# Second MLP matmul of a two-layer encoder: weight sums by accumulating DMA, and seven products for its last piece too

## The chip, the cores and the metric

One core of a Trainium2 chip. The time is that of one execution on the device, in microseconds (us): the median of three executions, and beside it one execution that the hardware profiler recorded.

## The reference

Two encoder layers on 512 tokens of 1024 features in fp32. Each layer is a token mixer (dilated window attention in layer 0, latent attention in layer 1) and a dense MLP with 4096 hidden units. The change touches the MLP alone, above all its second product:

```
def sq_relu_mlp(h, w1, w2):
    a = jax.nn.relu(h @ w1)
    return (a * a) @ w2

x = x + y                      # y: the mixer's output
h = rms_norm(x, norm_ffn[i])
x = x + sq_relu_mlp(h, ffn_w1[i], ffn_w2[i])
```

After layer 0 the next mixer begins with a norm over the 1024 features of each token, so it needs whole rows of `x`.

## The kernel before

Every matmul of two fp32 matrices is made from three matmuls in a shorter format (fp32r): each operand is split into a rounded part (`hi`, a copy on ScalarE) and a remainder (`lo`, a subtraction on VectorE), and hi x hi, hi x lo and lo x hi are added up in PSUM. So each piece of 128 x 1024 weights or activations costs one ScalarE copy and one VectorE subtraction before TensorE can use it. For the weights these are L157 and L158 (`load_unit`) or L523 and L524 (`split_w`, in `wino`); for the activations of the second MLP matmul L485 and L486 (`split_a`). Tiles named `whi`, `wlo` and `asp` hold the results. `whi` and `wlo` have four buffers each, `asp` four, raw weights three.

The MLP runs in four chunks of 1024 hidden units. `up(ch, grp)` makes one half chunk of hidden units from the normed input (matmuls L184, 192 of 128 x 512 for a half chunk); at its end four groups of 128 hidden units leave PSUM one after the other, each by a relu (L604) and a square (L605) on ScalarE, into the tile `a2`. `down(ch)` multiplies a chunk's `a2` by its 1024 x 1024 piece of the second weight matrix and adds the result to the residual `resid`. The order of the pieces is written out in `mlp`: two halves of `up(0)`, then for chunks 0 to 2 the first half of the next `up`, `down` of this chunk, the second half of the next `up`; at the end `down_last(3)`.

`down` is `wino` (L489): a 2 x 2 block scheme with seven products of half size (256 tokens x 512 hidden x 512 columns) in place of eight. Each product is 24 matmuls of 128 x 512, made in PSUM banks `sc` (chain a) or `tp` (chains b and d). `Aq(i, j)` is the block of token half i and hidden half j. The table `ORDER` lists the products, whether they open a bank or go on in it, and which block of `resid` gets the bank added afterwards (L553). The left sides of products 5, 6, 3 and 7 are sums or differences of blocks (L518, tile `S`); the weight sides of products 5, 6, 7 and 4 are differences of weight blocks, made by VectorE in place (L513, eight operations of 128 x 1024 for each `wino`). The weights come by eight DMAs of 512 KB from SyncE's queue into the four slots of `wqs`.

`down_last(3)` multiplies the last chunk directly: 192 matmuls (L184), in two column halves. All four left sides are split blocks of `a2`, hidden half 0 first. In the second column half the four token tiles end one after the other: L631 adds a tile to `resid` and calls `done(r, c)`. In layer 0 `done` is `done0`, which, for c = 1, norms the tile for the next mixer (`norm_tile`: mean square on ScalarE L136, a small add on VectorE L128, a power on GpSimd L131, the product L212 on VectorE, eight transposes on TensorE L123 into two `tp` banks, and each bank read by a ScalarE copy L220 and a VectorE subtraction L221). In layer 1 `done` sends the block to the output.

Behind layer 0's MLP the next mixer begins: its first weights (`w_in`, 896 elements in a row of a unit), and small tables `cgB` and `sgB` made by GpSimd (L699 to L701) from a gain `gr` that is loaded once TensorE is done with the last `up`.

A scheduler places the instructions of each engine in an order of its own, from the program's order and a model of costs; an engine runs its instructions in that order.

Of the kernel before, what the change touches and what calls it, by code (L numbers as in the profile page):

```python
# [13 lines left out]
ALU = mybir.AluOpType  # L14
# [73 lines left out]
def encoder_kernel(ctx: ExitStack, tc: tile.TileContext, x, norm_mix, norm_ffn, a_w_qkv, a_q_gain, a_k_gain,  # L88
# [394 lines left out]
    def split_a(x, pool):  # L483
        t = pool.tile([P, 4, 2, 256], F32R, tag="asp", name=nm("asp"), bufs=4)
        A.activation(t[:, :, 0], x, AF.Copy)  # L485
        V.tensor_tensor(t[:, :, 1], x, t[:, :, 0].bitcast(F32), op=ALU.subtract)  # L486
        return t

    def wino(tag, Aq, w, wqs, pool, resid):  # L489

        v = w.rearrange("(k p) c -> p k c", p=P)
        raw, S = {}, {}

        def load(key, slot):
            ki, ni = key  # L500
            raw[key] = []
            for u in range(2):
                t = wqs[:, 2 * slot + u]
                k0 = 4 * ki + 2 * u
                nc.sync.dma_start(t, v[:, k0:k0 + 2, 512 * ni:512 * ni + 512])
                raw[key].append(t)
        for key, slot in zip(((0, 0), (0, 1), (1, 1), (1, 0)), SLOTS[tag % 2]):
            load(key, slot)
        b11, b12, b22, b21 = raw[0, 0], raw[0, 1], raw[1, 1], raw[1, 0]

        def sub(o, x, y):
            for u in range(2):
                V.tensor_tensor(o[u], x[u], y[u], op=ALU.subtract)  # L513

        def stmp(name, x, y, op):
            if name not in S:
                S[name] = pool.tile([P, 4, 256], F32, tag="S", name=nm("S"), bufs=2)
            V.tensor_tensor(S[name], x, y, op=op)  # L518

        def split_w(x):  # L520
# [3 lines left out]
            V.tensor_tensor(lo, x, hi.bitcast(F32), op=ALU.subtract)  # L524
            return hi, lo

        def operands(p):
            if p == 1:
                return Aq(0, 0), b11
            if p == 5:  # L530
                stmp("c", Aq(1, 0), Aq(1, 1), ALU.add)
                sub(b11, b12, b11)
                return S["c"], b11
            if p == 6:
                stmp("c", S["c"], Aq(0, 0), ALU.subtract)
                sub(b11, b22, b11)
                return S["c"], b11
            if p == 3:
                stmp("c", Aq(0, 1), S["c"], ALU.subtract)
                return S["c"], b22  # L540
            if p == 7:
                stmp("d", Aq(0, 0), Aq(1, 0), ALU.subtract)
                sub(b12, b22, b12)
                return S["d"], b12
            if p == 2:
                return Aq(0, 1), b21
            sub(b11, b21, b11)
            return Aq(1, 1), b11

        def add_to(i, n, banks):  # L550
            for t in range(2):
                sl = resid[:, 2 * i + t, 512 * n:512 * n + 512]
                V.tensor_tensor(sl, sl, banks[t], op=ALU.add)  # L553

        banks = {}
        for p, chain, first, adds in ORDER:
# [6 lines left out]
            for u in range(2):  # L563
                hi, lo = split_w(wq[u])
                for t in range(2):
                    for j in range(2):
                        k = 2 * u + j
                        ah = at[:, k, 0, t * P:(t + 1) * P]
                        al = at[:, k, 1, t * P:(t + 1) * P]
                        for i, (lt, rt) in enumerate(((ah, hi), (ah, lo), (al, hi))):  # L570
                            PE.matmul(bk[t], lhsT=lt, rhs=rt[:, j], start=(first and k == 0 and i == 0),  # L571
                                      stop=(k == 3 and i == 2), skip_group_check=True)
            for i, n in adds:
                add_to(i, n, bk)

    SLOTS = ((0, 1, 2, 3), (2, 1, 3, 0))

    ORDER = [(1, "a", True, [(0, 0)]), (5, "b", True, [(1, 1)]), (6, "a", False, [(0, 1)]),
             (3, "b", False, [(0, 1)]), (7, "a", False, [(1, 1)]), (2, "d", True, [(0, 0)]), (4, "a", False, [(1, 0)])]

    def mlp(layer, w1, w2, hT_m, resid, pool, done):
        a2s = {}
# [26 lines left out]
        def down(ch):  # L609
            a2 = a2s.pop(ch)  # L610
            wino(layer * 4 + ch, lambda i, j: a2[:, 4 * j:4 * j + 4, 256 * i:256 * i + 256],
                 w2[1024 * ch:1024 * ch + 1024, :], wqs, pool, resid)

        def down_last(ch):

            a2 = a2s.pop(ch)
            at = {}
            for j in range(2):
                for i in range(2):
                    at[i, j] = split_a(a2[:, 4 * j:4 * j + 4, 256 * i:256 * i + 256], pool)  # L620

            def mm(r, kt, hi, lo, hv):
                t = at[r // 2, kt // 4][:, kt % 4]
                ah, al = (t[:, c, (r % 2) * P:(r % 2) * P + P] for c in range(2))
                sl = slice(0, 512)
                return [(ah, hi, sl), (ah, lo, sl), (al, hi, sl)]

            for c in range(2):
                def evac(r, acc, c=c):
                    sl = resid[:, r, 512 * c:512 * c + 512]  # L630
                    V.tensor_tensor(sl, sl, acc, op=ALU.add)  # L631
                    done(r, c)
                run_block(w_units(w2[1024 * ch:1024 * ch + 1024, :], 512 * c, 512), [1] * 4 if c == 0 else [4], 512,
                          mm, evac)
# [321 lines left out]
```

## Time and profile before

| | us |
|---|---|
| median of three executions | 1455.67 (1455.12 to 1456.37) |
| the profiled execution | 1457.98 |
| its span, first to last instruction | 1456.2 |
| TensorE busy | 1422.8 |
| VectorE busy | 903.5 |
| ScalarE busy | 710.3 |
| GpSimd busy | 117.4 |

The profile names the engines PE (TensorE matmul), PEld (its weight loads), DVE (VectorE), ACT (ScalarE), POOL (GpSimd) and SP (SyncE, which issues the DMAs). A row of the timeline has the start, the length of one or of several instructions that follow each other, engine, line, operation, output and inputs, the count, and in brackets the idle time ahead and what ended it. A row of a group has, behind the bar, its busy time, the mean length of one in ns, and the idle time ahead with its causes. "L184" is line 184 of the kernel.

### The profile page before, as it was taken

The numbers are of one execution on the slowest core, as the hardware profiler recorded it, in microseconds if no ns is written. First come the engines' busy times: TensorE is split into PE (matmuls) and PEld (weight loads), VectorE is DVE, ScalarE is ACT, GpSimd is POOL, SyncE is SP. The second block draws the span as 40 slices with busy tenths as digits, with TensorE's granted clock in tenths as the row PEclk, the third lists the DMA queues.
The fourth block names the chain that finished last, engine by engine and source line by source line (L and its number), as shares of the span: only waits on it lengthen the run. The fifth ranks groups of instructions, "written<-read, shape, count | busy, mean of one in ns | idle before, by whom it ended". The sixth has DMA issues, their size and how long they took to land.

```text
span 1456.2 us, 19181 instructions
## 1 busy us (share of the span) xinstructions
PE 1422.8 (98%) x7164; PEld 1210.6 (83%) x7164; DVE 903.5 (62%) x1431; ACT 710.3 (49%) x1572; POOL 117.4 (8%) x133
## 2 busy tenths in 40 slices
PE   7999999999999999999999999999999999999998
PEld 6889889889988878888888888776778888888887
DVE  6765466556437655285776835688754286675832
ACT  5544455355335533553644543787633453544530
POOL 1120120011011100000000010322100000000000
PEclk9999999999999999999999999999999999999999
DMA  6325114322531334415151032300014305151031
GB/s 227 102 55 167 59 46 131 102 63 58 171 94 58 95 130 157 147 36 171 40 174 58 15 111 68 97 30 30 30 44 162 127 30 173 44 172 61 7 111 72
DMA packets 113053, 135.58 MB, mean 93 GB/s; under 512 B 7488, under 2 KB 72256, under 8 KB 112960
## 3 DMA queue, kind: packets, MB, share of 16 engines
q1 hardware_dynamic: 112960, 134.35, 29.5%
q8 instruction: 57, 0.93, 0.3%
q14 instruction: 36, 0.29, 0.1%
HBM read 130.13 MB, written 4.19 MB: 92 GB/s over the span
## 4 chain that ended last, share of the span: by engine, by line
PE 94%; ACT 3%; DVE 2%; issue 1%; DMA 0%; POOL 0%; SPq 0%; DVEq 0%; ACTq 0%
PE acc L184 64%; PE sc L571 9%; PE tp L571 7%; PE tp L123 4%; PE acc L867 1%; PE sc L761 1%; PE acc L843 1%; PE sco L440 1%; PE sco L444 1%; PE sc L351 1%; PE sc L843 1%; DVE wlo L158 1%; PE sc L344 0%; PE tp L867 0%; PE sc L340 0%
## 5 line engine op out<-in xcount | busy, mean ns | idle before, releaser
L184 PE MATMUL acc<-whi,hT 128*128 128x512 f32 (+2 forms) x1600 | 486.5, 379 | 5.5 <-DVE t L311 2.2
L158 DVE TENSOR_TENSOR wlo<-raw,whi 128x1024 fp32r<-128x1024 f32 (+3 forms) x186 | 215.3, 1162 | 297.5 <-ACT whi L157 296.5
L157 ACT ACTIVATE whi<-raw 128x1024 fp32r<-128x1024 f32 (+3 forms) x186 | 187.2, 1010 | 317.8 <-PE acc L184 256.6
L184 PEld LDWEIGHTS acc<-whi,hT 128*128 128x128 f32 x1600 | 296.3, 189 | 47.1 <-issue 2.9
L184 PE MATMUL acc<-hT_f,whi 128*128 128x512 f32 (+1 forms) x1152 | 322.7, 367 | 1.7 <-DVE resid L650 1.2
L184 PE MATMUL acc<-wlo,hT 128*128 128x512 f32 (+2 forms) x800 | 299.9, 375 | 0.0
L184 PEld LDWEIGHTS acc<-hT_f,whi 128*128 128x128 f32 x1152 | 209.1, 189 | 37.4 <-DVE resid L650 1.6
L184 PE MATMUL acc<-hT_f,wlo 128*128 128x512 f32 (+1 forms) x576 | 208.3, 366 | 0.0
L184 PEld LDWEIGHTS acc<-wlo,hT 128*128 128x128 f32 x800 | 151.3, 189 | 19.9 <-DVE wlo L158 0.5
L523 ACT ACTIVATE whi<-wqs 128x1024 fp32r<-128x1024 f32 x84 | 89.2, 1062 | 110.2 <-PE sc L571 42.6
L184 PEld LDWEIGHTS acc<-hT_f,wlo 128*128 128x128 f32 x576 | 109.0, 189 | 17.5
L571 PE MATMUL sc<-whi,asp 128*128 128x512 f32 x384 | 122.1, 389 | 0.0
L524 DVE TENSOR_TENSOR wlo<-wqs,whi 128x1024 fp32r<-128x1024 f32 x84 | 102.6, 1222 | 25.9 <-ACT whi L523 25.8
L131 POOL TENSOR_TENSOR qrs<-rs_v,nhalf 128x4 f32<-128x4 f32 x48 | 61.5, 1290 | 408.3 <-DVE rs_v L128 393.8
L571 PE MATMUL tp<-whi,asp 128*128 128x512 f32 x288 | 91.6, 389 | 0.0
L571 PEld LDWEIGHTS sc<-whi,asp 128*128 128x128 f32 x384 | 72.1, 188 | 14.9
L184 PE MATMUL acc<-whi,asp 128*128 128x512 f32 x256 | 78.9, 389 | 0.0
L571 PE MATMUL sc<-wlo,asp 128*128 128x512 f32 x192 | 74.7, 389 | 0.0
L571 PEld LDWEIGHTS tp<-whi,asp 128*128 128x128 f32 x288 | 54.0, 188 | 11.2
L136 ACT ACTIVATE junk<-acc 128x128 f32<-128x128 f32 x192 | 53.0, 276 | 18.9 <-PE acc L184 13.9
L513 DVE TENSOR_TENSOR wqs<-wqs 128x1024 f32<-128x1024 f32 x48 | 58.0, 1219 | 0.2
L184 PEld LDWEIGHTS acc<-whi,asp 128*128 128x128 f32 x256 | 48.1, 188 | 10.0
(191 smaller groups left out, 1895.4 us busy)
## 6 DMA issues: line engine op xcount, KB each, us to landing
raw<-in_ffn_w_dram SPq DMA_DIRECT2D x80, 512.0 KB, 3.7
raw<-in_a_w_qkv_dram SPq DMA_DIRECT2D x96, 256.0 KB, 3.4
wqs<-in_ffn_w_dram SPq DMA_DIRECT2D x48, 512.0 KB, 4.4
raw<-in_a_w_qkv_dram SPq DMA_DIRECT2D x64, 192.0 KB, 2.8
raw<-in_a_w_o_dram SPq DMA_DIRECT2D x8, 512.0 KB, 4.1
raw<-in_b_w_o_dram SPq DMA_DIRECT2D x8, 512.0 KB, 3.7
xt<-in_x_dram SPq DMA_DIRECT2D x8, 256.0 KB, 5.6
vd<-vt SPq DMA_DIRECT2D x8, 256.0 KB, 3.5
```

The lines of the kernel that those rows point to most:

```text
L123: PE.transpose(o, i, ident)
L131: G.tensor_tensor(out, v[:, :n], nhalf[:, :n], op=ALU.pow)
L136: A.activation(junk, x, AF.Square, scale=1.0 / math.sqrt(dim), accum_out=out)
L157: A.activation(hi[:, :nk, :n], raw[:, :nk, :n], AF.Copy)
L158: V.tensor_tensor(lo[:, :nk, :n], raw[:, :nk, :n], hi[:, :nk, :n].bitcast(F32), op=ALU.subtract)
L184: PE.matmul(accs[o][:, oc], lhsT=lt, rhs=rt, start=(kt == 0 and p_i == 0 and hv == 0), stop=(kt == total - 1 and p_i == 2), skip_group_che ...
L351: PE.matmul(sc[:, r * P:(r + 1) * P], lhsT=qT[:, r * P:(r + 1) * P], rhs=kT[:, r * P:(r + 1) * P], start=True, stop=True)
L513: V.tensor_tensor(o[u], x[u], y[u], op=ALU.subtract)
L523: A.activation(hi, x, AF.Copy)
L524: V.tensor_tensor(lo, x, hi.bitcast(F32), op=ALU.subtract)
L571: PE.matmul(bk[t], lhsT=lt, rhs=rt[:, j], start=(first and k == 0 and i == 0), stop=(k == 3 and i == 2), skip_group_check=True)
L843: PE.matmul(sc, lhsT=lt, rhs=rt, start=(i == 0), stop=(i == 4))
```

## The change

`wino` gets another set of seven products in another order (5, 1, 3, 6, 7, 2, 4), in which every weight side is a single block or a sum of two blocks with positive signs. The signs move to the left sides (four operations, L517) and to the adds to `resid`, which are now adds or subtractions (`put`, L554). A sum of two weight blocks is no longer made on VectorE: one block is loaded by SyncE's queue as before (L511), and the other is added onto it in SBUF by a DMA that accumulates, issued by GpSimd (`accum_op`, L509). Each `wino` now has ten loads by SyncE and eight accumulating DMAs by GpSimd, each of 512 KB; the eight subtractions of L513 are gone. Slot `sT` of `wqs` is summed onto three times: (0,0)+(0,1) for product 5, then (1,1) for product 6 and (1,0) for product 4, each once the split of the product before is done. The slots change places in a round of four.

`down_last` is removed; the last chunk goes through `wino` too, with `done` passed on. For this call product 4 runs token tile by token tile (`tail`), and `done` is called at each final add (after products 6, 7, 2 and 4); `done0` now norms a tile at its second call.

```diff
-        def operands(p):
-            if p == 1:
-                return Aq(0, 0), b11
-            if p == 5:
-                stmp("c", Aq(1, 0), Aq(1, 1), ALU.add)
-                sub(b11, b12, b11)
-                return S["c"], b11
...
-            sub(b11, b21, b11)
-            return Aq(1, 1), b11
+        def fetch(slot, key, add=False):
...
+                if add:
+                    nc.gpsimd.dma_start(t, src, accum_op=ALU.add)
+                else:
+                    nc.sync.dma_start(t, src)
...
+        sT, s1, s3, s7 = slots
+        fetch(sT, (0, 0))
+        bT = fetch(sT, (0, 1), add=True)
+        b1 = fetch(s1, (0, 0))
+        b3 = fetch(s3, (1, 1))
+        fetch(s7, (0, 1))
+        b7 = fetch(s7, (1, 1), add=True)
+
+        def operands(p):
+            if p == 5:
+                return stmp("c", Aq(1, 0), Aq(1, 1), ALU.subtract), bT
+            if p == 1:
+                return Aq(0, 0), b1
+            if p == 3:
+                stmp("d", S["c"], Aq(0, 0), ALU.subtract)
+                return stmp("c", S["d"], Aq(0, 1), ALU.add), b3
+            if p == 6:
+                return S["d"], fetch(sT, (1, 1), add=True)
+            if p == 7:
+                return stmp("c", Aq(0, 0), Aq(1, 0), ALU.subtract), b7
+            if p == 2:
+                return Aq(0, 1), fetch(s1, (1, 0))
+            return Aq(1, 1), fetch(sT, (1, 0), add=True)
+
+        def put(i, n, op, banks):
             for t in range(2):
                 sl = resid[:, 2 * i + t, 512 * n:512 * n + 512]
-                V.tensor_tensor(sl, sl, banks[t], op=ALU.add)
+                V.tensor_tensor(sl, sl, banks[t], op=op)
+                if done is not None and p in (2, 4, 6, 7):
+                    done(2 * i + t, n)
...
+            tail = done is not None and p == 4
+            parts = {}
+            for u, t in ((0, 0), (1, 0), (0, 1), (1, 1)) if tail else ((0, 0), (0, 1), (1, 0), (1, 1)):
...
-    ORDER = [(1, "a", True, [(0, 0)]), (5, "b", True, [(1, 1)]), (6, "a", False, [(0, 1)]),
-             (3, "b", False, [(0, 1)]), (7, "a", False, [(1, 1)]), (2, "d", True, [(0, 0)]), (4, "a", False, [(1, 0)])]
+    ORDER = [(5, "b", True, (1, 1, ALU.add)), (1, "a", True, (0, 0, ALU.add)), (3, "b", False, (0, 1, ALU.add)),
+             (6, "a", False, (0, 1, ALU.subtract)), (7, "a", False, (1, 1, ALU.subtract)),
+             (2, "d", True, (0, 0, ALU.add)), (4, "a", False, (1, 0, ALU.add))]
...
-        def down_last(ch):
...
-        down_last(3)
+        down(3)
...
         def done0(r, c):
-            if c == 0:
+            state[r] = state.get(r, 0) + 1
+            if state[r] < 2:
                 return
```

Two places show what moves. The first is the end of layer 0's last `up`. TensorE before (`acc_1204` is the last tile of `up`, `asp_1217` a split left side of hidden half 0):

```order
L184 MATMUL acc_1204_7224<-hT_f0_4965,wlo_1216_7318 128x512
L184 MATMUL acc_1204_7224<-hT_f0_4965,whi_1215_7317 128x512 x2
L184 MATMUL acc_1204_7224<-hT_f0_4965,wlo_1216_7318 128x512
L184 MATMUL acc_1221_7365<-whi_1226_7371,asp_1217_7353 128x512
L184 MATMUL acc_1221_7365<-wlo_1227_7372,asp_1217_7353 128x512
```

TensorE now (`asp_1218` is product 5's left side, `asp_1225` product 1's; `tp` and `sc` are the banks of their chains):

```order
L184 MATMUL acc_1204_7230<-hT_f0_4965,whi_1215_7323 128x512 x2
L184 MATMUL acc_1204_7230<-hT_f0_4965,wlo_1216_7324 128x512
L578 MATMUL tp_1219_7376<-whi_1221_7378,asp_1218_7373 128x512
L578 MATMUL tp_1219_7376<-wlo_1222_7379,asp_1218_7373 128x512
L578 MATMUL tp_1220_7377<-whi_1221_7378,asp_1218_7373 128x512
L578 MATMUL tp_1220_7377<-wlo_1222_7379,asp_1218_7373 128x512
L578 MATMUL sc_1226_7415<-whi_1228_7417,asp_1225_7412 128x512
```

ScalarE at the same place, before (`a2_1141` holds the last chunk's activations, L157 copies weights):

```order
L157 ACTIVATE whi_1235_7461<-raw_1234_7459 128x1024
L604 ACTIVATE a2_1141_6801<-acc_1204_7224 128x512
L605 ACTIVATE a2_1141_6801<-a2_1141_6801 128x512
L485 ACTIVATE asp_1219_7359<-a2_1141_6801 128x4x256
L485 ACTIVATE asp_1220_7362<-a2_1141_6801 128x4x256
```

ScalarE now (relu and square are L615 and L616; `S_1217` is product 5's difference):

```order
L523 ACTIVATE whi_1230_7433<-wqs_955_5335 128x1024
L615 ACTIVATE a2_1141_6801<-acc_1204_7230 128x512
L616 ACTIVATE a2_1141_6801<-a2_1141_6801 128x512
L485 ACTIVATE asp_1218_7373<-S_1217_7371 128x4x256
L485 ACTIVATE asp_1225_7412<-a2_1141_6801 128x4x256
```

Before, the first left side behind `up` was split long ago; now it is the one that is made last, behind relu, square and VectorE's difference, and TensorE's four matmuls of product 5 stand ahead of product 1's.

The second place is the end of layer 0's MLP on VectorE, before (L631 adds a finished token tile, L212 is the norm's product, L221 the remainder of a transposed bank):

```order
L631 TENSOR_TENSOR resid_4957<-resid_4957,acc_1237_7493 128x512
L128 TENSOR_SCALAR rs_v_1257_7552<-nss_1255_7549 128x1
L212 SCALAR_TENSOR_TENSOR xn_1256_7550<-resid_4957,nrs_1258_7554,g_mix1_1253_7546 128x1024
L631 TENSOR_TENSOR resid_4957<-resid_4957,acc_1238_7494 128x512
L128 TENSOR_SCALAR rs_v_1263_7599<-nss_1261_7596 128x1
L212 SCALAR_TENSOR_TENSOR xn_1262_7597<-resid_4957,nrs_1264_7601,g_mix1_1253_7546 128x1024
L631 TENSOR_TENSOR resid_4957<-resid_4957,acc_1239_7495 128x512
L221 TENSOR_TENSOR hT_1254_7548<-tp_1259_7557,hT_1254_7548 128x4x128
```

VectorE now (`tp_1249`, `tp_1250` are product 2's banks, `sc_1226`, `sc_1227` product 4's; `wlo_1298`, `wlo_1301` and `w0` are weights of the next mixer):

```order
L554 TENSOR_TENSOR resid_4957<-resid_4957,tp_1250_7574 128x512
L158 TENSOR_TENSOR wlo_1295_7782<-raw_1293_7779,whi_1294_7781 128x2x448
L128 TENSOR_SCALAR rs_v_1259_7614<-nss_1257_7611 128x1
L554 TENSOR_TENSOR resid_4957<-resid_4957,sc_1226_7415 128x512
L128 TENSOR_SCALAR rs_v_1265_7637<-nss_1263_7634 128x1
L212 SCALAR_TENSOR_TENSOR xn_1258_7612<-resid_4957,nrs_1260_7616,g_mix1_1255_7608 128x1024
L212 SCALAR_TENSOR_TENSOR xn_1264_7635<-resid_4957,nrs_1266_7639,g_mix1_1255_7608 128x1024
L158 TENSOR_TENSOR wlo_1298_7788<-raw_1296_7785,whi_1297_7787 128x2x448
L554 TENSOR_TENSOR resid_4957<-resid_4957,sc_1227_7416 128x512
L158 TENSOR_TENSOR w0_7768<-raw_1334_7993,w0_7768 128x512
L158 TENSOR_TENSOR wlo_1301_7794<-raw_1299_7791,whi_1300_7793 128x2x448
L221 TENSOR_TENSOR hT_1256_7610<-tp_1261_7619,hT_1256_7610 128x4x128
```

And TensorE there now (L123 are transposes, the `acc_1286` rows the next mixer's first matmuls):

```order
L578 MATMUL sc_1227_7416<-whi_1272_7671,asp_1269_7658 128x512
L123 MATMUL tp_1261_7619<-ck_89,xn_1258_7612 128x128 x4
L123 MATMUL tp_1262_7626<-ck_89,xn_1258_7612 128x128 x4
L184 MATMUL acc_1286_7769<-whi_1291_7775,hT_1256_7610 128x448
L184 MATMUL acc_1286_7769<-wlo_1292_7776,hT_1256_7610 128x448
L123 MATMUL tp_1267_7642<-ck_89,xn_1264_7635 128x128 x4
```

The norm products of tiles 0 and 1 moved from between the adds of the last matmuls to behind product 4's first add, and the bank's remainder behind four more operations.

More of the change, by code (lines that the diff above doesn't have):

```diff
@@ L562, in wino @@
             bk = banks[chain]
[L563 to L576, printed above, removed]
-    ORDER = [(1, "a", True, [(0, 0)]), (5, "b", True, [(1, 1)]), (6, "a", False, [(0, 1)]),
-             (3, "b", False, [(0, 1)]), (7, "a", False, [(1, 1)]), (2, "d", True, [(0, 0)]), (4, "a", False, [(1, 0)])]
+            tail = done is not None and p == 4
+            parts = {}
+            for u, t in ((0, 0), (1, 0), (0, 1), (1, 1)) if tail else ((0, 0), (0, 1), (1, 0), (1, 1)):
+                if u not in parts:
+                    parts[u] = split_w(wq[u])
+                hi, lo = parts[u]
+                for j in range(2):
+                    k = 2 * u + j
+                    ah = at[:, k, 0, t * P:(t + 1) * P]
+                    al = at[:, k, 1, t * P:(t + 1) * P]
+                    for i_, (lt, rt) in enumerate(((ah, hi), (ah, lo), (al, hi))):
+                        PE.matmul(bk[t], lhsT=lt, rhs=rt[:, j], start=(first and k == 0 and i_ == 0),
+                                  stop=(k == 3 and i_ == 2), skip_group_check=True)
+            put(i, n, op, bk)
+    SLOTS = [(0, 1, 2, 3)]
+    for _ in range(3):
+        t_, p_, q_, r_ = SLOTS[-1]
+        SLOTS.append((q_, r_, p_, t_))
+    ORDER = [(5, "b", True, (1, 1, ALU.add)), (1, "a", True, (0, 0, ALU.add)), (3, "b", False, (0, 1, ALU.add)),
+             (6, "a", False, (0, 1, ALU.subtract)), (7, "a", False, (1, 1, ALU.subtract)),
+             (2, "d", True, (0, 0, ALU.add)), (4, "a", False, (1, 0, ALU.add))]
     def mlp(layer, w1, w2, hT_m, resid, pool, done):
@@ L611, in down @@
             wino(layer * 4 + ch, lambda i, j: a2[:, 4 * j:4 * j + 4, 256 * i:256 * i + 256],
-                 w2[1024 * ch:1024 * ch + 1024, :], wqs, pool, resid)
-        def down_last(ch):
[L616 to L634, printed above, removed]
+                 w2[1024 * ch:1024 * ch + 1024, :], wqs, pool, resid, done if ch == 3 else None)
         up(0, 0)
```

32 lines of the change are left out of this document (7 added, 25 removed).

## The prediction

> **What bounds the kernel now.** The first view is the page's own head: busy time of each engine, and the chain that ended last, by engine.
>
> ```profile
> span 1456.2 us, 19181 instructions
> PE 1422.8 (98%) x7164; PEld 1210.6 (83%) x7164; DVE 903.5 (62%) x1431; ACT 710.3 (49%) x1572; POOL 117.4 (8%) x133
> PE 94%; ACT 3%; DVE 2%; issue 1%; DMA 0%; POOL 0%; SPq 0%; DVEq 0%; ACTq 0%
> ```
>
> TensorE works for 98% of the span, and the chain of waits is TensorE for 94%. So matmuls taken away are time taken away, unless a new wait fills their place. The second view is that chain in order of time, at the end of layer 1 (start, length, what).
>
> ```profile
> 1305.37 43.52 PE acc L184 x192
> 1348.89 5.44 PE sc L571 x24
> ...
> 1386.97 65.29 PE acc L184 x288
> ```
>
> One of the seven products is 24 matmuls in 5.44 us, 0.2267 us each. The 288 at the end are 96 of the last `up` and the 192 of `down_last`, in one piece: TensorE passes from `up` to the last piece of the second matmul without a wait. The third view is the busy time of each engine in chosen stretches: one `down` by seven products, layer 0's `down_last`, the change to the next mixer, and what follows the last matmul.
>
> ```profile
> 638.60:676.70 38.10, 38.10 (x170) 31.55 (x169) 32.26 (x34) 19.66 (x20) 0.00 (x0) 1.00 0.45 138
> 861.70:905.30 43.60, 43.60 (x198) 36.14 (x198) 19.69 (x23) 14.91 (x20) 8.84 (x12) 1.00 0.20 58
> 905.00:935.00 30.00, 29.88 (x164) 26.77 (x163) 21.81 (x55) 19.65 (x62) 6.60 (x11) 1.00 0.43 127
> 1452.30:1456.20 3.90, 0.00 (x0) 0.00 (x0) 0.68 (x1) 0.00 (x0) 0.00 (x0) 1.00 0.18 67
> ```
>
> After the length come PE, PEld, DVE, ACT and POOL busy; the last three numbers are granted clock, DMA share and GB/s. TensorE is full in all three stages, VectorE has 6 us to spare in a `down`, and the tail is 3.90 us.
>
> **The six earlier `down`s.** 48 weight subtractions leave VectorE (8 in each of six), which had time to spare there: worth nothing. The new first product reads both hidden halves of the activations, but half of another `up` stands between their making and it. Its sums now come by DMA; that risk is a rival below.
>
> **The last `down`, matmuls.** 192 become 7 x 24 = 168: 24 x 0.2267 = 5.44 us less in each layer, 10.88 in all.
>
> **The last `down`, its first wait.** TensorE's first rows are now product 5, whose left side is a VectorE difference that needs all of the last `up`. Product 1, ready earlier, stands behind it. The timeline at the end of layer 0's last `up` shows what has to pass first.
>
> ```profile
> 861.29 0.39 PE L184 MATMUL acc<-hT_f,wlo 128*128 128x512 f32 x1
> 861.52 0.39 PE L184 MATMUL acc<-whi,asp 128*128 128x512 f32 x1
> 861.52 1.04 ACT L157 ACTIVATE whi<-raw 128x1024 fp32r<-128x1024 f32 x1
> 862.47 0.58 ACT L604 ACTIVATE a<-acc 128x512 f32<-128x512 f32 x1
> 863.09 0.63 ACT L605 ACTIVATE a<-a 128x512 f32<-128x512 f32 x1
> ```
>
> Call 861.52 T. Before, the next matmul starts at T, for its operand came from the older half. The relu of the last tile runs only from T+0.95, behind a weight copy that itself waits for TensorE's last matmul (its buffer); its square ends at T+2.20. ScalarE's order keeps this: one weight copy, relu, square, then product 5's copy. What follows costs by the groups of the second half of layer 0:
>
> ```profile
> L518 DVE TENSOR_TENSOR S<-a 128x1024 f32<-128x1024 f32 x6 | 7.1, 1222 | 0.0
> L485 ACT ACTIVATE asp<-S 128x1024 fp32r<-128x1024 f32 x12 | 12.6, 1054 | 7.1 <-DVE S L518 7.1
> ```
>
> The difference ends at 2.20+1.22 = T+3.42, the copy at T+4.5, and with a hand-over of some 0.1 us at each of three steps TensorE starts near **T+4.75**. Less than 4.0 (relu 0.58, square 0.63, 1.22, 1.05 and hand-overs, with nothing ahead of the relu) can't be had by this order; more than 5.5 has no reason.
>
> **What a wait does to the clock.** The trace has waits of half this length. One, with the granted clock (third number from the end) in the stretches behind it:
>
> ```profile
> 93.79 0.41 PE L184 MATMUL acc<-whi,hT 128*128 128x384 f32 x1 [2.24 <-DVE t L311]
> ...
> 95.00:96.00 1.00, 1.00 (x6) 1.00 (x5) 1.00 (x2) 0.97 (x5) 0.00 (x0) 0.62 0.81 241
> 96.00:97.00 1.00, 1.00 (x5) 1.00 (x4) 1.00 (x4) 0.14 (x2) 0.00 (x0) 0.50 0.07 21
> 97.00:98.00 1.00, 1.00 (x5) 1.00 (x4) 1.00 (x3) 0.00 (x0) 0.81 (x1) 0.50 0.73 214
> 98.00:99.00 1.00, 1.00 (x6) 1.00 (x5) 1.00 (x2) 0.00 (x0) 1.00 (x1) 0.67 0.55 163
> ```
>
> A wait of 2.24 us was followed by a half clock: 0.38+0.50+0.50+0.33 = 1.7 us of clock lost while TensorE was full. I charge **1.7** for each wait of over 2 us. A 4.75 us wait may lose more (a second such stretch, 3.4) or, if the half clock falls mostly into the wait itself, 1.0. The Trainium skill, "TensorE: Matmul & The Clock Gate", Part 1, says that the clock halves after an idle window of about 3.4 us that runs freely, and comes back after as long a busy one. By that, estimated, a 4.75 us wait holds a whole idle window in 4 cases of 10, so 0.7 us on average, and the sum would be some 3 to 4 us less; the trace's 2.24 us wait speaks against so high a bar.
>
> **The last `down`, VectorE.** It now makes seven left sides' remainders, eleven weight remainders, four differences and the adds in one go. From the third left side (about T+9.2, after product 3's difference and its copy) until the remainder that product 2 begins with, its order has 13 operations of 1024 and 6 of 512 elements. Their cadence:
>
> ```profile
> 649.38 1.22 DVE L524 TENSOR_TENSOR wlo<-wqs,whi 128x1024 fp32r<-128x1024 f32 x1
> 650.51 1.28 DVE L553 TENSOR_TENSOR resid<-resid,tp 128x512 f32<-128x512 f32 x2
> 651.71 1.22 DVE L524 TENSOR_TENSOR wlo<-wqs,whi 128x1024 fp32r<-128x1024 f32 x1
> ```
>
> So 13 x 1.13 + 6 x 0.60 = 18.3 us: ready at T+27.5. TensorE gets there after four products and two matmuls: 4.75 + 98 x 0.2267 = 27.0, plus 1.7 by the clock = T+28.7. No wait in layer 1 (0.8 at full clock; by the shown lengths, 13 x 1.22 + 6 x 0.68, the most is 2.2). Layer 1's tail keeps its 3.90 us: an add and a store behind the last matmul, as now. **Layer 1: -5.44+4.75+1.7 = +1.0.**
>
> **Layer 0, GpSimd.** Here the next mixer's small tables fall into the same stretch.
>
> ```profile
> 862.10 0.42 SPq L692 DMA_DIRECT2D gr<-in_b_k_gain_dram  x1
> 864.74 0.47 POOL L699 TENSOR_TENSOR cgB<-ck,gr 128x128 f32<-128x128 f32 x1 [290.58 <-DMA gr<-in_b_k_gain_dram]
> 864.85 2.84 DVE L486 TENSOR_TENSOR asp<-a,asp 128x1024 fp32r<-128x1024 f32 x2 [1.02 <-ACT asp L485]
> 865.16 1.44 POOL L700 TENSOR_TENSOR sgB<-ck,gr 128x128 f32<-128x128 f32 x1
> ```
>
> Two VectorE operations took 2.84 instead of 1.22+1.13 = 2.35, and GpSimd's 0.47 became 1.44: they take turns, 0.49 for each. From T+3.2 the eight table products now alternate with the four VectorE operations ahead of product 3's left side: 4 x 0.5 = 2.0 later (between 0 and 8 x 0.49 = 3.9). Product 2's remainder then comes at T+29.6 against 28.7: **0.9** of wait (0 to 2.8). GpSimd's last two weight sums stand behind these tables, but aren't wanted before product 4, some 15 us on.
>
> **Layer 0, its end.** Before, column half 1 ended tile by tile, so that norms ran under matmuls:
>
> ```profile
> 895.36 0.68 DVE L631 TENSOR_TENSOR resid<-resid,acc 128x512 f32<-128x512 f32 x1
> 898.08 1.28 DVE L212 SCALAR_TENSOR_TENSOR xn<-resid,nrs,g_mix 128x1024 f32<-128x1024 f32 x1 [0.66 <-POOL nrs L131]
> 905.97 1.03 PE L123 MATMUL tp<-ck,xn 128*128 128x128 f32 x8
> 906.61 1.08 ACT L220 ACTIVATE hT<-tp 128x512 fp32r<-128x512 f32 x2 [0.80 <-PE tp L123]
> ```
>
> Add to normed tile took 4.0 us. Now tiles 0 and 1 are final only after product 2, 5.44 us before the end E of product 4, and VectorE's row puts the adds of both, then one of product 4 (done at E-2.7), ahead of the two norm products: these run about E-1.8 to E+0.6. Tile 0's transposes start near E, its copy lets two matmuls go at E+1.25, done by E+1.65. Then the row wants tile 1's transposes, into a bank that tile 0's remainder frees; ahead of that on VectorE stand, from E+0.6, two weight remainders of 896 (1.0 each, taken from 1.13), an add and a remainder of 512 (0.6 each) and itself: E+0.6+3.2+0.6 = E+4.4. Waits 0.2+2.8 = **3.0**, between 1.3 (if only what follows the last add counts) and 4.4; and again **1.7** of clock. **Layer 0: -5.44+4.75+1.7+0.9+3.0+1.7 = +6.6.**
>
> **Sum:** +1.0+6.6 = +7.6, on the profiled 1457.98 (span 1456.2 and 1.78 around it) 1465.6; the median is 2.31 lower, so 1455.67+7.6 = **1463.3**.
>
> **Rivals.** *No change.* The clock term is smaller and layer 0's end is caught up: two first waits of 4.75 and two of 1.0 for the clock against 10.88 give +0.6, with a shorter end +2: 1456 to 1458. For it: both extra terms of layer 0 rest on orders, not on rows of waits. Against: rows of half clock stand behind waits of 2.24 us.
>
> *Faster.* The place is the first wait: were the clock to stay at 1.00 and the chain to take its least, 4.0, with no other wait, 2 x (4.0-5.44) = -2.9: 1452.8. It decides once all waits together are under 8.0 us. Nothing but the order's slack speaks for it; two chains of 4.75 alone are 9.5.
>
> *The DMA sums come late.* The trace has no accumulating DMA and none from GpSimd; nearest:
>
> ```profile
> q1 hardware_dynamic: 112960, 134.35, 29.5%
> wqs<-in_ffn_w_dram SPq DMA_DIRECT2D x48, 512.0 KB, 4.4
> ```
>
> 134.35 MB in 29.5% of 1456.2 us is 313 GB/s while moving, 1.7 us for 512 KB, 4.4 to land. Product 4's sum can be issued once product 6's weights are split, about 2 us into product 6, and is wanted 2 us before product 4: 3 x 5.44-4 = 12 us for two. At half that rate (3.4 us each, 2.7 to land) they fit, also beside the next loads. At a third, with two loads ahead, they come some 4 us late; over six or eight `down`s 25 to 35 more: 1488 to 1498. The Trainium skill, "DMA: Bandwidth & Descriptors", Anatomy of one DMA — SWDGE (gpsimd) path, gives 2.0 us and 436 GB/s, an estimated 3.2 us for each: no wait; no run here shows it.
>
> *The sums are made in time, but issuing them holds GpSimd up:* a norm's power of the mixer before stands behind the first sum of each layer; 1 to 3 us, inside the range.
>
> **Chances.** A measurement of this kernel can tell 0.2%, 2.9 us. Forecast 0.66; no change 0.20; faster 0.04; late sums 0.10. Faster by over 0.2%: 0.04; within: 0.20; slower: 0.76. The likeliest case by itself spans 1459 (clock 1.0 a wait, end 1.3) to 1473 (3.4 for the long waits, end 4.4, second waits 2). The range takes in part of the no-change case below and a share of late sums above: 1456 to 1476.
>
> **What would show it.** Each step right: 168 matmuls in each last `down`; a TensorE wait of 4 to 5.5 us put down to ScalarE's copy of a left side at its start, and a clock of 0.50 behind it; no wait before product 2 in layer 1, a short one in layer 0; 2 to 4 us of waits at the mixer's first transposes; the six other `down`s still 38.1 us. Wrong: product 1 running in the first wait, a clock that stays 1.00, or TensorE waiting for GpSimd's DMAs.

## The result, and the profile after

The changed kernel takes 1465.33 us (median of four, 1464.91 to 1465.81) against 1455.74: ratio 1.0067, 95% interval 1.0054 to 1.0080, so 9.6 us slower. The profiled execution took 1465.81 us.

The page's head of the changed kernel, as before: span, busy time, and the chain that ended last.

```profile
span 1463.5 us, 19306 instructions
PE 1416.1 (97%) x7116; PEld 1203.2 (82%) x7116; DVE 888.2 (61%) x1421; ACT 727.0 (50%) x1590; POOL 197.3 (13%) x197
PE 91%; ACT 3%; DVE 3%; issue 2%; DMA 1%; POOL 0%; SPq 0%; DVEq 0%; ACTq 0%; POOLq 0%
```

TensorE has 48 matmuls less (7116) and is busy 6.7 us less, not 10.88, for some of them ran longer; and its share of the chain fell from 94 to 91%: it waits more. The chain in order of time at the end of layer 1 (start, length, what):

```profile
1393.97 20.87 PE acc L184 x92
1419.48 2.03 PE tp L578 x4
1421.51 1.65 PE sc L578 x4
1423.16 4.57 PE tp L578 x20
...
1454.03 5.45 PE sc L578 x24
```

Where 288 matmuls stood in one piece, there is a hole from 1414.9 to 1419.5, and the first eight matmuls behind it take 2.03 + 1.65 = 3.68 us instead of 8 x 0.2267 = 1.81. The timeline of the hole, ScalarE, VectorE and TensorE:

```profile
1414.89 1.04 ACT L523 ACTIVATE whi<-wqs 128x1024 fp32r<-128x1024 f32 x1
1415.84 0.58 ACT L615 ACTIVATE a<-acc 128x512 f32<-128x512 f32 x1
1415.97 1.23 DVE L524 TENSOR_TENSOR wlo<-wqs,whi 128x1024 fp32r<-128x1024 f32 x1 [4.23 <-ACT whi L523]
1416.45 0.63 ACT L616 ACTIVATE a<-a 128x512 f32<-128x512 f32 x1
1417.11 1.23 DVE L517 TENSOR_TENSOR S<-a 128x1024 f32<-128x1024 f32 x1
1418.37 1.06 ACT L485 ACTIVATE asp<-S 128x1024 fp32r<-128x1024 f32 x1 [1.29 <-DVE S L517]
1419.48 0.75 PE L578 MATMUL tp<-whi,asp 128*128 128x512 f32 x1 [4.43 <-ACT asp L485]
```

Weight copy, relu, square, difference, copy, first matmul: each starts about where the one before ends. The difference has a second row ahead of it, VectorE's weight remainder (L524), which waits for the same weight copy and ends at 1417.20, 0.1 us behind the square at 1417.08; the chain that ended last goes through it. Now the stretches of both last pieces and of the change to the next mixer (length, PE, PEld, DVE, ACT, POOL; then granted clock, DMA share, GB/s):

```profile
860.43:865.02 4.59, 0.16 (x2) 0.00 (x1) 3.48 (x3) 3.27 (x6) 1.35 (x2) 0.80 0.32 66
865.02:870.00 4.98, 4.98 (x12) 3.92 (x13) 4.44 (x4) 1.40 (x2) 4.98 (x5) 0.50 0.16 63
870.00:905.61 35.61, 35.61 (x159) 29.30 (x158) 30.37 (x35) 19.77 (x22) 7.31 (x8) 1.00 0.26 50
905.61:910.61 5.00, 1.71 (x11) 1.09 (x9) 5.00 (x7) 3.48 (x6) 0.00 (x0) 1.00 0.32 84
910.61:915.61 5.00, 5.00 (x21) 4.55 (x22) 3.36 (x5) 1.33 (x2) 0.55 (x1) 0.66 0.61 177
1414.89:1419.48 4.59, 0.16 (x1) 0.00 (x1) 3.48 (x3) 3.27 (x6) 0.00 (x0) 1.00 0.20 57
1419.48:1424.48 5.00, 5.00 (x15) 3.98 (x16) 3.88 (x5) 2.34 (x3) 0.00 (x0) 0.66 0.15 59
1424.48:1459.30 34.82, 34.82 (x155) 28.63 (x153) 26.30 (x29) 13.92 (x14) 2.44 (x2) 1.00 0.33 84
```

Twice 4.59 us pass until TensorE's next matmul (4.43 of them idle), and behind that the clock is 0.50 in layer 0 and 0.66 in layer 1 over 5 us; from then on TensorE is full to the end of the piece. In layer 0 the clock had already halved within the wait (0.80 over 4.59 us, so some 1.8 us at a half). The third hole, at the mixer's first transposes, has two waits, while VectorE works all the time (5.00 of 5.00): the first ends with ScalarE's copy of a bank, which stands behind weight copies of the next mixer, the second with VectorE's remainder. The rows of it:

```profile
905.47 1.28 DVE L212 SCALAR_TENSOR_TENSOR xn<-resid,nrs,g_mix 128x1024 f32<-128x1024 f32 x1 [0.44 <-POOL nrs L131]
906.61 0.93 ACT L157 ACTIVATE whi<-raw 128x896 fp32r<-128x896 f32 x1
907.45 1.07 ACT L220 ACTIVATE hT<-tp 128x512 fp32r<-128x512 f32 x2
908.08 0.47 PE L184 MATMUL acc<-whi,hT 128*128 128x448 f32 x1 [1.44 <-ACT hT L220]
910.61 0.82 PE L123 MATMUL tp<-ck,xn 128*128 128x128 f32 x4 [1.85 <-DVE hT L221]
```

The sums by DMA: their queue (packets, MB, share of 16 engines), and the issue list (queue, count, KB, us to landing):

```profile
q0 software_dynamic: 17408, 33.56, 14.1%
...
wqs<-in_ffn_w_dram SPq DMA_DIRECT2D x80, 512.0 KB, 4.9
...
wqs<-in_ffn_w_dram POOLq DMA_DIRECT2D x64, 512.0 KB, 7.4
```

7.4 us to landing, within the 12 that they have; in layer 0's last piece no copy of ScalarE waits for a DMA.

To compare runs, three lengths on TensorE, from start to start, are read off each timeline: (A) from the last matmul of layer 0's last `up` to the last matmul of layer 0's last piece; (B) from there to the last matmul of layer 1's last `up`; (C) the same as A in layer 1. Together they cover all that the change touches from the first last piece on; for the two kernels they are the differences of these rows' starts.

| | A | B | C | sum against before |
|---|---|---|---|---|
| before (861.29, 905.74, 1408.35, 1451.87) | 44.45 | 502.61 | 43.52 | |
| changed (860.20, 905.38, 1414.66, 1459.08) | 45.18 | 509.28 | 44.42 | +8.3 |

A before holds eight transposes (0.87 us in the chain: 43.58 without); in the changed kernel they fall into B. So layer 0's piece grew by 1.6, what follows by 5.8 (6.67 less those 0.87), layer 1's piece by 0.9. The rest up to 9.6 is how single executions differ: the profiled one of before was itself 2.3 us over its median.

### The profile page after: what moved, and what is told of

It is laid out like the page before. It is cut to its first block, busy times and chain, and to the rows that moved or that the text cites. A ratio compares the mean times of both kernels' runs of the same rounds, so it can differ in the third digit from the quotient of the medians.

```text
span 1463.5 us, 19306 instructions
## 1 busy us (share of the span) xinstructions
PE 1416.1 (97%) x7116; PEld 1203.2 (82%) x7116; DVE 888.2 (61%) x1421; ACT 727.0 (50%) x1590; POOL 197.3 (13%) x197
## 3 DMA queue, kind: packets, MB, share of 16 engines
q0 software_dynamic: 17408, 33.56, 14.1%
## 4 chain that ended last, share of the span: by engine, by line
PE 91%; DVE 3%; ACT 3%; issue 2%; DMA 1%; POOL 0%; SPq 0%; DVEq 0%; ACTq 0%; POOLq 0%
PE acc L184 57%; PE sc L578 12%; PE tp L578 9%; PE tp L123 4%; PE acc L857 1%; PE acc L833 1%; PE sc L751 1%; PE sco L444 1%; PE sco L440 1%; PE sc L351 1%; DVE wlo L158 1%; PE sc L833 1%; PE sc L344 0%; PE tp L857 0%; PE sc L340 0%
## 5 line engine op out<-in xcount | busy, mean ns | idle before, releaser
L158 DVE TENSOR_TENSOR wlo<-raw,whi 128x1024 fp32r<-128x1024 f32 (+3 forms) x170 | 195.8, 1156 | 241.1 <-ACT whi L157 236.3
L157 ACT ACTIVATE whi<-raw 128x1024 fp32r<-128x1024 f32 (+3 forms) x170 | 170.3, 1005 | 268.3 <-PE acc L184 170.8
L524 DVE TENSOR_TENSOR wlo<-wqs,whi 128x1024 fp32r<-128x1024 f32 x112 | 137.1, 1224 | 123.3 <-ACT whi L523 123.2
L523 ACT ACTIVATE whi<-wqs 128x1024 fp32r<-128x1024 f32 x112 | 118.8, 1060 | 170.4 <-PE sc L578 60.9
L578 PE MATMUL sc<-whi,asp 128*128 128x512 f32 x512 | 164.7, 391 | 0.0
L509 POOL DMA_DIRECT2D wqs<-in_ffn_w_dram x64 | 78.2, 1347 | 541.9 <-DVE wlo L524 283.9
L578 PE MATMUL tp<-whi,asp 128*128 128x512 f32 x384 | 125.1, 394 | 8.9 <-ACT asp L485 8.9
L578 PEld LDWEIGHTS sc<-whi,asp 128*128 128x128 f32 x512 | 96.7, 189 | 20.1
L578 PE MATMUL sc<-wlo,asp 128*128 128x512 f32 x256 | 100.5, 393 | 0.0
L578 PE MATMUL tp<-wlo,asp 128*128 128x512 f32 x192 | 75.9, 395 | 0.0
L578 PEld LDWEIGHTS sc<-wlo,asp 128*128 128x128 f32 x256 | 48.6, 190 | 10.3
```

Source lines behind the costliest of these rows:

```text
L157: A.activation(hi[:, :nk, :n], raw[:, :nk, :n], AF.Copy)
L158: V.tensor_tensor(lo[:, :nk, :n], raw[:, :nk, :n], hi[:, :nk, :n].bitcast(F32), op=ALU.subtract)
L509: nc.gpsimd.dma_start(t, src, accum_op=ALU.add)
```

## The experiments

Theory: the loss is (1) the first wait with the half clock behind it, in both layers, (2) layer 0's late norms. Rivals: the accumulating DMAs cost; any last piece of seven products loses; the slow first matmuls have another cause than the clock; GpSimd's tables. Every timed result is beside its own runs of the kernel before (1456.1 to 1456.4).

**Sums by DMA alone.** The direct last piece is put back in both layers.

```diff
-        down(3)
+        down_last(3)
```

> Only the first part of the change: the six earlier pieces use the new order and the sums by DMA, the last piece is the direct product again in both layers. Theory (the loss is made of waits at the last piece, half clock behind them and the end of layer 0): no change against before, 1455.7 +- 1.5 us, the six pieces 38.1 us each. Rival (the accumulating DMAs, or GpSimd's issuing of them, cost time): a third to all of the loss stays, 1459 to 1465 us.

Measured: 1456.20 against 1456.30, ratio 1.0004 (0.9995 to 1.0013). The earlier pieces still take 38.10 us; one of them, VectorE now 27.12 us busy instead of 32.26:

```profile
637.00:675.10 38.10, 38.10 (x170) 31.55 (x169) 27.12 (x29) 18.26 (x19) 7.29 (x6) 1.00 0.78 194
```

So the new order and the sums cost and bring nothing there that this run can tell (-0.7 to +1.9 us); the loss sits at the last piece and what follows it.

**The last piece by the old seven products,** with weight differences on VectorE: the kernel before with `down(3)`, the same token-tile end and `done`.

```diff
-        down_last(3)
+        down(3)
```

> Only the second part of the change, with the old scheme: the last piece by seven products too, token tile by token tile at its end, but with the old set of products (1, 5, 6, 3, 7, 2, 4) and weight differences on VectorE; no DMA sums. Product 1 needs only old activations. Theory: no wait at its start and no half clock there, so 10.88 us of matmuls are saved; the end of layer 0 still costs 3.3 of waits, 1.7 of clock and about 1.5 in the mixer, and VectorE, with eight more operations, 0 to 3 us for each layer: 1450 to 1457 us. Rival (any seven-product last piece loses at its start): 1462 to 1466 us.

Measured: 1463.17, ratio 1.0048 (1.0035 to 1.0060): a miss; the time is the rival's. The wait did move. VectorE's rows after the last `up` in layer 0, and TensorE's:

```profile
861.69 1.49 DVE L518 TENSOR_TENSOR S<-a 128x1024 f32<-128x1024 f32 x1
863.10 1.48 DVE L513 TENSOR_TENSOR wqs<-wqs 128x1024 f32<-128x1024 f32 x1
864.50 1.48 DVE L524 TENSOR_TENSOR wlo<-wqs,whi 128x1024 fp32r<-128x1024 f32 x1
...
867.84 1.22 PE L576 MATMUL tp<-whi,asp 128*128 128x512 f32 x2 [3.02 <-DVE asp L486]
```

Product 1 hides the relus, but then product 5's remainder stands behind a weight difference and a weight remainder: 3.02 us of wait, and a half clock. C is 43.55, as long as the direct piece, and B 510.78: the late norms again. That VectorE isn't free at this place is what this run shows; the sums by DMA can be worth something only here. With them and product 1 first C is 41.14 (next run), so not every last piece of seven products loses at its start; but that run has the other set of products too, so what the sums alone bring isn't shown.

**Product 1 first.** The changed kernel, two entries exchanged:

```diff
-    ORDER = [(5, "b", True, (1, 1, ALU.add)), (1, "a", True, (0, 0, ALU.add)), (3, ...
+    ORDER = [(1, "a", True, (0, 0, ALU.add)), (5, "b", True, (1, 1, ALU.add)), (3, ...
```

> The changed kernel with products 1 and 5 exchanged in the order table, nothing else. Theory: the two waits of 4.6 us and the half clock behind them (1.9 and 2.6 us) go, some waits on VectorE's remainders come in their place (0.5 to 2.5 us in each layer): 1452 to 1457 us, 8 to 13 us under the changed kernel. Rival (the loss sits elsewhere, the wait only moves to product 5): over 1461 us.

Measured: 1465.06, ratio 1.0061 (1.0047 to 1.0075): a miss in the time, which is the rival's. By stages it is half right: C falls from 44.42 to 41.14, 2.4 under the direct piece; but A rises to 46.40. In layer 0, GpSimd, ScalarE and TensorE:

```profile
871.26 1.19 POOL L509 DMA_DIRECT2D wqs<-in_ffn_w_dram  x1
877.36 2.01 ACT L523 ACTIVATE whi<-wqs 128x1024 fp32r<-128x1024 f32 x2 [5.73 <-DMA wqs<-in_ffn_w_dram]
885.74 0.73 PE L578 MATMUL tp<-whi,asp 128*128 128x512 f32 x2 [2.89 <-ACT whi L523]
```

Product 6's sum is issued only behind GpSimd's tables, ScalarE stands 5.73 us for it, and TensorE 2.89 behind the copies queued there. The rows are those of the fastest execution: 1460.80 at a mean granted clock of 0.997, while the other four took 1463.8 to 1465.7 at 0.992 to 0.995. A mean of 0.004 less over 1460 us is, estimated, 5.8 us, so the half clock can account for the difference; there are no rows of those four to show it.

**The wait filled.** Twenty matmuls of 512 columns on a constant tile ahead of product 5 of each last piece; their result isn't used.

```diff
+        if done is not None:
+            jk = acc_p.tile([P, 512], F32, tag="acc", name=nm("jk"))
+            for q in range(20):
+                PE.matmul(jk[:64], lhsT=fill, rhs=fill.unsqueeze(1).broadcast_to([P, 8, 64]), start=(q == 0), stop=(q == 19))
```

> The changed kernel with 20 matmuls of 512 columns on a constant tile put ahead of product 5 in the last piece of each layer; their result is not used. They fill 4.5 of the 4.6 us that TensorE waits. Theory (the wait makes the granted clock fall to a half): the clock stays at 1.00 there and the 1.9 and 2.6 us behind the waits come back although TensorE does more work: 1460 to 1462 us. Rival (the slow first products have another cause, such as operands that come late): 1465 to 1467 us.

Measured: 1465.29, ratio 1.0062 (1.0050 to 1.0075): the time is the rival's, the trace is the theory's. The stretches behind the fill in both layers, and two waits that the changed kernel doesn't have:

```profile
864.55:869.55 5.00, 5.00 (x22) 3.98 (x22) 4.53 (x4) 1.40 (x3) 5.00 (x5) 1.00 0.18 68
1418.82:1423.82 5.00, 5.00 (x23) 3.98 (x22) 3.87 (x5) 2.34 (x4) 0.00 (x0) 1.00 0.16 61
```

```profile
889.02 0.50 PE L584 MATMUL tp<-wlo,asp 128*128 128x512 f32 x1 [1.43 <-DVE wlo L526]
1442.03 0.50 PE L584 MATMUL tp<-wlo,asp 128*128 128x512 f32 x1 [0.59 <-DVE wlo L526]
```

The clock is 1.00 where it was 0.50 and 0.66, with 22 and 23 matmuls in 5 us instead of 12 and 15: the idle time is what halves it. But TensorE then stands for VectorE's remainder at product 2. In layer 0 that product's first matmul with a weight remainder starts 29.0 us after the last `up` (889.02 - 860.01) here and 29.25 in the changed kernel (889.68 - 860.43). A is 45.00 and C 43.79, only 0.2 and 0.6 less. The half clock was covering a wait on VectorE, so its net price in the last piece is under 1 us for each layer, not 1.9 and 2.6. The expectation had left out what the prediction's own sum held.

**One layer at a time.** Seven products in layer 1's last piece only, then in layer 0's only.

```diff
-        down(3)
+        (down if layer == 1 else down_last)(3)
```

> The changed kernel with the direct last piece in layer 0 and seven products in layer 1 only. Theory (the trace of the changed kernel: 44.6 us for layer 1's last piece against 43.5): 1.1 us over the kernel before, 1456.5 to 1458.5 us. Rival (the loss is the same in both layers, half of 9.6): about 1460.5 us.

> The changed kernel with seven products in layer 0's last piece and the direct one in layer 1. Theory: all of layer 0's loss stays (first wait, half clock, late norms, the mixer behind them), 7 to 8.5 us over the kernel before: 1463 to 1465 us. Rival (the loss is the same in both layers): about 1460.5 us.

Measured: 1457.77, ratio 1.0010 (1.0001 to 1.0018), and 1464.25, 1.0056 (1.0043 to 1.0069), both as expected: 1.7 and 8.1 us, which add up to 9.8 beside 9.6. The loss is layer 0's by five to one.

**Product 2 before 7.** The changed kernel, two other entries exchanged, so that token tiles 0 and 1 are final one product earlier.

```diff
-             ... (7, "a", False, (1, 1, ALU.subtract)), (2, "d", True, (0, 0, ALU.add)), (4, ...
+             ... (2, "d", True, (0, 0, ALU.add)), (7, "a", False, (1, 1, ALU.subtract)), (4, ...
```

> The changed kernel with products 2 and 7 exchanged in the order table, so that token tiles 0 and 1 are final one product (5.44 us) earlier and their norms can run under matmuls. Theory (the late norms cost 3.3 us of waits, 1.7 of half clock and some 1.5 in the mixer behind): the first wait of 4.4 us stays in both layers, the two waits at the mixer's first transposes go down to under 1 us together, 4 to 6 us less than the changed kernel: 1459 to 1462 us. Rival (the late norms are not what costs there): 1464 to 1466 us.

Measured: 1461.05, ratio 1.0036 (1.0023 to 1.0048), 4.3 us under the changed kernel, as expected. The change to the mixer, in one stretch:

```profile
895.00:915.00 20.00, 19.94 (x104) 17.09 (x103) 17.17 (x24) 11.65 (x20) 3.25 (x4) 1.00 0.34 98
```

TensorE is full through it at a clock of 1.00; B is 503.66 instead of 509.28. With A (46.20, the transposes within), layer 0 costs 2.8 us instead of 7.4. The late norms are shown.

**Product 1 first, in layer 1 only.**

```diff
-    ORDER = [(5, "b", True, (1, 1, ALU.add)), (1, "a", True, (0, 0, ALU.add)), (3, ...
+    ORDER = [(1, "a", True, (0, 0, ALU.add)), (5, "b", True, (1, 1, ALU.add)), (3, ...
...
-        down(3)
+        (down if layer == 1 else down_last)(3)
```

> Product 1 first, direct last piece in layer 0, seven products in layer 1 only. Theory (in the run with product 1 first, layer 1's last piece took 41.3 us against 43.5): 2 us under the kernel before, 1453.5 to 1455 us. Rival (the waits on VectorE bring a half clock in most executions and take the gain back): 1455.5 to 1457.5 us.

Measured: 1454.71, ratio 0.9991 (0.9982 to 1.0000); C is 41.13. The time is inside the theory's range, 1.4 us under its own runs of the kernel before where 2 were expected; the interval just reaches no change.

**All together.** Both exchanges in the table, which now begins 1, 5, 3, 6, 2, 7, 4, without and with GpSimd's tables queued behind the last sum:

```diff
-    ORDER = [(5, ...), (1, ...), (3, ...), (6, ...), (7, ...), (2, ...), (4, ...)]
+    ORDER = [(1, ...), (5, ...), (3, ...), (6, ...), (2, ...), (7, ...), (4, ...)]
...
+            with tc.issue_after(last_sum[0]):
                 for t in range(2):
                     for hf in range(2):
...
-                    nc.gpsimd.dma_start(t, src, accum_op=ALU.add)
+                    last_sum[0] = nc.gpsimd.dma_start(t, src, accum_op=ALU.add).ins
```

> Both exchanges in the order table (product 1 first, product 2 before 7), and in layer 0 GpSimd's tables for the next mixer queued behind the last weight sum. Theory (losses are the first wait, the late norms, and with product 1 first the tables that stand ahead of the sums in GpSimd's queue): the 10.88 us of matmuls are saved in good part, layer 0's last piece about 42.3 us with its transposes (44.45 before), 1.1 us lost behind it, layer 1's 41.1 against 43.5: 1451 to 1454.5 us, under both kernels. Rival (what is taken from one wait comes back in the next): over 1456 us.

> Both exchanges in the order table, GpSimd's tables left where they were. Theory: product 6's and 4's sums again stand behind the tables in layer 0, a TensorE wait of about 3 us for a weight copy there and a half clock after it in most executions, 3 to 6 us over the kernel with the tables late: 1456 to 1459.5 us. Rival (the tables don't matter): equal to the kernel with the tables late within 1 us.

Measured: 1453.34 with the tables late, ratio 0.9984 (0.9975 to 0.9993); 1452.53 with the tables in their place, 0.9978 (0.9969 to 0.9987). The first as expected, the second a miss: the tables don't matter here. In its trace ScalarE waits 5.02 us for product 6's sum too, but a left side's copy that stood behind that wait with product 1 alone now stands ahead of it, and TensorE has no wait there; this is read from the rows, not tried. C is 40.16, A 43.08. The two ScalarE rows, and what waits remain at product 5 in both layers and in layer 0's transposes:

```profile
871.46 1.04 ACT L485 ACTIVATE asp<-a 128x1024 fp32r<-128x1024 f32 x1
877.52 2.01 ACT L523 ACTIVATE whi<-wqs 128x1024 fp32r<-128x1024 f32 x2 [5.02 <-DMA wqs<-in_ffn_w_dram]
...
866.35 0.74 PE L578 MATMUL tp<-whi,asp 128*128 128x512 f32 x2 [1.49 <-DVE asp L486]
894.62 1.09 PE L123 MATMUL tp<-ck,xn 128*128 128x128 f32 x8 [0.95 <-DVE xn L212]
...
1412.15 0.74 PE L578 MATMUL tp<-whi,asp 128*128 128x512 f32 x2 [1.13 <-DVE asp L486]
```

Two exchanges in the order table turn 9.6 us slower into 3.8 us faster than before; nothing else differs between the changed kernel and this one. That is the version that beats both.

**Product 1 first with the tables late, and the changed kernel with the tables late.** The edits are the exchange of products 1 and 5 with the last edit above, and the last edit above alone.

> Product 1 first (products 2 and 7 in their places) and GpSimd's tables behind the last sum. Theory: against the run with product 1 first alone (1465.1 us, layer 0's last piece 46.4 us) the wait of 2.9 us for the late sum goes, layer 0's piece falls to 41 to 42.5 us; the late norms (5.8 us) stay: 1456 to 1459.5 us. Rival (the sums weren't late because of the tables): 1463 to 1466 us.

> The changed kernel with only GpSimd's tables moved behind the last sum. Theory: in the changed kernel the half clock behind the first wait covers what GpSimd takes from VectorE, so nothing is gained but perhaps part of layer 0's longer half clock: 1463.5 to 1466 us. Rival (VectorE's turns with GpSimd cost 2 us or more there): 1462 to 1463.5 us.

Measured: 1458.86, ratio 1.0019 (1.0011 to 1.0028), and 1466.03, 1.0071 (1.0059 to 1.0084). With product 1 first, A falls from 46.40 to 41.87 once the sums don't stand behind the tables: that wait is shown to be theirs. In the changed kernel the same move brings nothing (A 45.13 against 45.18), since the half clock covers it.

| | A | B | C | sum against before | measured against before |
|---|---|---|---|---|---|
| changed | 45.18 | 509.28 | 44.42 | +8.3 | +9.6 |
| old seven | 44.97 | 510.78 | 43.55 | +8.7 | +6.9 |
| product 1 first | 46.40 | 508.65 | 41.14 | +5.6 | +8.8 |
| filled | 45.00 | 509.27 | 43.79 | +7.5 | +9.0 |
| product 2 before 7 | 46.20 | 503.66 | 44.44 | +3.7 | +4.9 |
| product 1 first, tables late | 41.87 | 509.88 | 41.14 | +2.3 | +2.5 |
| both exchanges | 43.08 | 503.08 | 40.16 | -4.3 | -3.8 |

A trace is one execution; the two columns differ by up to 3.2 us where long waits are left (with product 1 first the traced execution was the fastest), and by under 1 where few are.

## Why the prediction was right, point by point

The direction, the time and most of the mechanism were right: 1463.3 forecast, 1465.33 measured, range 1456 to 1476. Where single terms were off, some of them cancelled.

- *Matmuls.* 168 in each last piece: right.
- *First wait.* T+4.75 forecast, 4.59 in both layers, through the very rows named. Right. One row was overlooked: VectorE's weight remainder ends 0.1 us behind the square and stands ahead of the difference too, so by these rows taking away only what is ahead of the relu would have left the wait nearly as long (not tried).
- *Clock.* 1.7 for each long wait: in layer 1, 44.42 - 38.08 - 4.59 = 1.75. In layer 0 2.5 (45.18 - 38.08 - 4.59), behind a wait of the same length: some 6.8 us at a half, twice layer 1's 3.4, of which 1.8 fell into the wait. The second stretch is what the forecast had named as the larger case (3.4). That the idle time is the cause is shown by the filled run. The same run shows that the term can't be added to the others as it stands: at full clock the forecast's own figures give -5.44 + 4.75 + 0.8 = +0.1 for layer 1, and the filled run 43.79 - 43.52 = +0.3.
- *The bar for the clock.* In all eight such waits of the profiled runs (two each in the changed kernel, with product 2 before 7 and with the tables late, one each with one layer at a time) the 5 us behind ran at a mean granted clock of 0.50 to 0.66. The Trainium skill's bar, a whole idle window that runs freely ("TensorE: Matmul & The Clock Gate", Part 1), would have halved the clock in some 3 of 10 waits of this length, an estimate from that page's 3.4 us: (4.4 - 3.4) / 3.4. Eight of eight speak for a lower bar. But a fixed charge for each wait of over 2 us, as in the forecast, is more than the runs bear out: the wait of 2.2 to 2.6 us near 92 us was followed by a half clock in 8 of the 14 profiled kernels, the one of 2.1 us near 524 us only in the kernel before.
- *VectorE up to product 2.* Ready at T+27.5 in layer 1 by the forecast; 1442.03 - 1414.29 = T+27.7 where the fill lays it bare. TensorE forecast at T+28.7, found at 1443.44 - 1414.89 = T+28.6: no wait. Right. Layer 0: VectorE at T+29.6 forecast (27.5 + 2.0 is 29.5, and the wait then 0.8), T+29.0 found; the wait did not come, since the clock had cost 0.8 more there. That these two cancel in the sum is in part luck: nothing in the forecast said that layer 0 would get the second stretch of half clock. What GpSimd takes from VectorE was mis-sized by some 0.6 and did not matter (with the tables late A is 45.13 against 45.18).
- *Layer 1:* +1.0 forecast, +0.9 in the trace, +1.7 (0.1 to 2.6) measured by itself.
- *Layer 0's end.* Waits of 3.0 forecast, 1.44+1.85 = 3.3 found, but otherwise split: the first, taken as 0.2, was 1.44, because ScalarE's copy of the bank stood behind weight copies of the next mixer (two matmuls go at E+2.5 instead of E+1.25, and tile 1's transposes at E+5.0 instead of E+4.4, with E at 905.61). Half clock 1.7: 5 x (1.00 - 0.66) = 1.7. So this place took 5.0 of the 5.8. The balance over all of B is another: TensorE's idle time grew by 4.7 us, from 12.1 (502.61 with 490.49 busy) to 16.8 (509.28 with 492.47 busy), so 1.4 of waits that nobody charged come later in the mixer. The half clock adds next to nothing on balance in these two executions, for each has two stretches of 3.4 us in B, before near 940 and 1117 us, now near 913 and 947. Some 1 us (5.8 - 4.7) stays open. The term was too small, 4.7 against 5.8, and that it came so near is in part luck: waits that it left out stand where it charged the clock.
- *DMA sums late:* not in the changed kernel. At 33.56 MB in 14.1% of 1463.5 us they move 163 GB/s, half the rate of the loads, the case that the prediction let fit. The median landed in 7.4 us, not in the 2.7 of that case or the 3.2 that the prediction estimated besides, but still in time. But in the run with product 1 first they did come late, not by their own time but by what stood ahead of them on GpSimd; the rival was right that sums can come late and wrong in its cause.
- *Sum.* +7.6 forecast, +8.3 in the trace, +9.6 between medians; the 1.3 between the last two is not traced to a place.

## What to carry to other kernels

Fewer matmuls are worth their time only if the first of them can start: before taking out a block, look at what the first new matmul reads, and put first the product that reads the oldest data. The same holds at the end: the block that somebody waits for goes first, not last. And a wait that disappears beside a half clock or a slower neighbour brings only the distance to the next engine's own time, so price each one with the others removed.

## What the runs showed of the hardware

- After 4.43 us of idle TensorE (4.59 from the last matmul's slot to the next start), 12 matmuls in 5 us at a granted clock of 0.50, against 22 with the idle time filled by matmuls that do nothing.
- 64 accumulating DMAs of 512 KB: 7.4 us to landing (4.9 for plain loads beside them), 1.35 us of GpSimd to issue each (mean of 64; 78.2 us busy in all, as some overlap, by the group's row below). With 48 of them beside six pieces in which TensorE is full the time was the same (1.0004, 0.9995 to 1.0013).

```profile
L509 POOL DMA_DIRECT2D wqs<-in_ffn_w_dram x64 | 78.2, 1347 | 541.9 <-DVE wlo L524 283.9 <-DMA wqs<-in_ffn_w_dram 242.1 <-ACT xn L136 8.7
```

- In the changed kernel the half clock came in stretches of about 3.4 us or twice that: 0.66 over 5 us in layer 1, and in layer 0 0.80 over 4.59 us and 0.50 over the next 4.98. A wait of 4.4 us was followed by it in eight of eight cases, one of 2.2 to 2.6 us in 8 of 14, one of 2.1 us in 1 of 14.
- Executions of one kernel spread differently, and the length of the waits alone does not settle it: 0.9 us among four of the changed kernel and 1.2 among five with the tables late, both with waits of 4.4 us, but 4.9 with product 1 first and 5.0 with product 2 before 7 (mean granted clock 0.992 to 0.997), against 3.2 to 3.9 among the 15 to 27 of the kernel before. What sets the spread stays open.
